# Queries and keys of three attention groups by seven products instead of eight

## The chip, the cores and the metric

One core of one Trainium2 chip. The metric is the device time of one execution in microseconds. TensorE (PE in the profile, its weight loads PEld), VectorE (DVE), ScalarE (ACT), GpSimd (POOL) and SyncE (SP) run side by side, each through its own queue in order, and wait for each other by semaphores.

## The reference

Two decoder layers over 256 tokens of width 2048. The change concerns the first one's differential attention:

```
q, k, v = split(h @ wqkv, 3)          # h: rms-normed x, wqkv: 2048 x 6144
q, k    = partial_rope(heads of 128)  # 16 heads, in 8 pairs
a       = softmax(q0 k0') - lam * softmax(q1 k1')   # per pair, causal
x       = x + rms_norm(a @ v, subln) * 0.2 @ wo
```

The second layer has multi-head latent attention. After each attention come a cross-attention into 256 memory tokens and a squared-ReLU feed-forward block of width 8192, and at the end a norm. All in float32.

## The kernel before, in words

**Precision.** Each float32 operand is split into two fp32r halves, and a product takes three matmuls: high x high, high x low, low x high. Weights come in tiles of 128x2048 floats (1 MB, pool `wraw`, tiles named `raw`, 6 buffers): 512 rows of the contraction by 512 columns. `split_pieces.next` makes of half such a tile `whi` (a cast on ScalarE, L193) and `wlo` (a subtraction on VectorE, L194). `whi` and `wlo` have 4 buffers each, so two weight tiles' worth of halves exist at a time.

**Activations** lie transposed in `unit` tiles (four 128-row pieces, both halves; 13 buffers). With 256 tokens there are two token blocks t = 0, 1. `matmul_chunk` computes 512 output columns for both blocks: 16 row pieces x 2 blocks x 3 = 96 matmuls, named `mm`.

**Attention in groups.** Differential attention runs in 4 groups of 512 columns (2 pairs of heads). `project_diff` takes the chunks for queries, keys and values; `heads_T` scales and rotates queries and keys (rotation on GpSimd, L454 to L459), transposes them on TensorE (L159) and splits them into `unit` tiles. `attend_diff` is a side task: for three blocks of scores it does softmax (L492) and weights (`a`, L631, L632), transposes these, multiplies by values, and then norms and transposes. While a group's side task runs, the main line does the output projection of the group before (`da_wo`, 4 tiles) and the projections of the group after (12 tiles).

**Order.** TensorE's order is as the program emits it. A model clock (`mmul` adds to it) decides between main-line matmuls which step of a side task is emitted: a task yields how long to wait (`T_SM` 6.5 us and so on), and `pump` emits steps that are due. A list `plan` sets the order of weight tiles, at most 4 ahead. The other engines' orders are set by a scheduler when the program is built. Weight loads go on SP's queue in the program's order.

**Seven products.** The feed-forward block's up projection already uses a Strassen-Winograd scheme (`Seven`): token blocks times halves of the contraction on one side, halves of the contraction times two chunks on the other, seven products p1 to p7 in place of eight, each of 8 row pieces x 3 = 24 matmuls (named `pr`) in two items x = 0, 1 of one weight tile. Sums of weights are made on VectorE (p5, p7; L758, 128x2048) or by a load that adds onto a tile, on GpSimd's queue (p6, p4; L764). Sums of activations s1 to s4 come from `Forms` (L412 sums, L384 and L385 halves). Outputs are put together on VectorE (L793). A product's item takes 12 matmuls, a plain one 24.

## Time and profile before

| | |
|---|---|
| median of 3 runs | 2247.61 us (2247.14 to 2247.9) |
| profiled execution | 2249.26 us, span 2247.5 us, granted clock 0.998 |
| PE busy | 2228.2 us, 99% |
| DVE busy | 1675.6 us, 75% |
| ACT busy | 1354.6 us, 60% |
| group 1, 62 to 153.5 us | PE 91.50, DVE 52.62, ACT 47.87 us busy |
| one feed-forward period, 620 to 704.4 us | PE 84.21, DVE 69.29, ACT 53.40 us busy |

The stretch from 62 us has the values of the first group, its attention and the projections of the second; those from 153.5 and 248 us the two groups after. In a row of a stretch stand its bounds and length, then busy time and number of instructions of PE, PEld, DVE, ACT and POOL, the granted clock, the share of the DMA engines and GB/s. A row of the timeline has start, duration, engine, line, operation, output and inputs, count, and in brackets the idle time before it and what ended it. A group row has count, busy time and mean duration in ns, then the idle time before.

### The profile page before, as it was taken

The page shows a single profiled execution, that of the slowest core. Times are in us where ns is not written, and L with a number is a line of the kernel's source. Part 1 is how long each engine was busy: PE and PEld are TensorE (multiplying, and loading weights), DVE is VectorE, ACT ScalarE, POOL GpSimd, SP SyncE. Part 2 cuts the span into 40 slices and gives each one's busy share as a digit, 9 for nine tenths or more (in the row PEclk, how much of TensorE's full clock was granted, in tenths as well). Part 3 has the DMA queues.
Part 4 walks back from the last instruction along what each step waited for, and adds up shares of the span by engine and source line. Part 5 has one row for each costly group of instructions (what it writes and reads, how often), then busy time and mean ns, then how long its engine had stood idle before and what let it go on. Part 6 is the DMA issues. An engine that isn't in the chain of part 4 may idle for free.

```text
span 2247.5 us, 27444 instructions
## 1 busy us (share of the span) xinstructions
PE 2228.2 (99%) x10521; PEld 1853.7 (82%) x10521; DVE 1675.6 (75%) x1836; ACT 1354.6 (60%) x1815; POOL 153.9 (7%) x250
## 2 busy tenths in 40 slices
PE   9999999999999999999999999999999999999998
PEld 7888888888888888888889888888888888888786
DVE  6665647678888788788765766778887887887864
ACT  6544645666666666656655755566666666666664
POOL 0210110000000000000000311000000000000001
PEclk9999999999999999999999999999999999999999
DMA  9446555435877877876955334643688678678692
GB/s 364 157 143 210 193 197 206 152 129 206 262 250 254 244 249 255 244 249 219 297 176 180 116 141 150 243 150 132 216 255 277 222 250 275 223 250 276 221 306 75
DMA packets 73716, 484.09 MB, mean 215 GB/s; under 512 B 8432, under 2 KB 8816, under 8 KB 18032
## 3 DMA queue, kind: packets, MB, share of 16 engines
q1 hardware_dynamic: 64944, 422.56, 50.9%
q0 software_dynamic: 8064, 58.72, 13.1%
q8 instruction: 82, 1.34, 0.2%
q10 hardware_dynamic: 576, 1.05, 0.2%
q14 instruction: 50, 0.41, 0.1%
HBM read 480.20 MB, written 2.10 MB: 215 GB/s over the span
## 4 chain that ended last, share of the span: by engine, by line
PE 92%; DVE 5%; ACT 2%; issue 1%; DMA 0%; ACTq 0%; POOLq 0%
PE mm L155 66%; PE pr L155 20%; PE ax L155 3%; PE ax L159 2%; DVE wlo L194 2%; DVE raw L758 2%; ACT whi L193 1%; PE mm L159 1%; DVE unit L289 0%; DMA raw<-in_da_wqkv_dram 0%; DVE x L438 0%; DVE unit L316 0%; ACT ev L1078 0%; DVE unit L487 0%; DVE os L658 0%
## 5 line engine op out<-in xcount | busy, mean ns | idle before, releaser
L194 DVE TENSOR_TENSOR wlo<-raw,whi 128x1024 fp32r<-128x1024 f32 (+2 forms) x962 | 1154.6, 1213 | 483.6 <-ACT whi L193 455.2
L193 ACT CAST whi<-raw 128x1024 fp32r<-128x1024 f32 (+2 forms) x962 | 993.6, 1041 | 754.5 <-PE mm L155 530.9
L155 PE MATMUL mm<-whi,unit 128*128 128x512 f32 (+3 forms) x4544 | 1444.0, 389 | 2.6 <-ACT unit L315 1.7
L155 PEld LDWEIGHTS mm<-whi,unit 128*128 128x128 f32 x4544 | 850.1, 188 | 169.2 <-ACT unit L315 2.7
L155 PE MATMUL mm<-wlo,unit 128*128 128x512 f32 (+3 forms) x2272 | 878.3, 387 | 2.2 <-DVE wlo L194 2.2
L155 PE MATMUL pr<-whi,unit 128*128 128x512 f32 x1568 | 502.9, 391 | 0.0
L155 PEld LDWEIGHTS mm<-wlo,unit 128*128 128x128 f32 x2272 | 428.0, 188 | 85.6 <-DVE wlo L194 7.2
L155 PEld LDWEIGHTS pr<-whi,unit 128*128 128x128 f32 x1568 | 294.4, 188 | 61.3 <-ACT whi L193 0.5
L155 PE MATMUL pr<-wlo,unit 128*128 128x512 f32 x784 | 307.3, 392 | 3.0 <-DVE wlo L194 2.7
L155 PEld LDWEIGHTS pr<-wlo,unit 128*128 128x128 f32 x784 | 147.2, 188 | 39.5 <-DVE wlo L194 9.5
L758 DVE TENSOR_TENSOR raw<-raw,raw 128x2048 f32<-128x2048 f32 x56 | 127.9, 2284 | 0.0
L764 POOL DMA_DIRECT2D raw<-in_mlp_wup_dram x56 | 49.4, 882 | 1125.6 <-DVE wlo L194 990.3
L438 DVE TENSOR_TENSOR x<-x,mm 128x512 f32<-128x512 f32 x152 | 100.0, 682 | 9.4 <-PE mm L155 8.7
L328 POOL TENSOR_TENSOR rs<-rs,mhalf 128x1 f32<-128x1 f32 (+1 forms) x28 | 23.5, 844 | 681.5 <-DVE rs L327 681.5
L288 ACT CAST unit<-ax 128x512 fp32r<-128x512 f32 (+1 forms) x88 | 48.9, 567 | 30.1 <-PE ax L159 27.7
L289 DVE TENSOR_TENSOR unit<-ax,unit 128x512 fp32r<-128x512 f32 (+1 forms) x88 | 57.4, 661 | 3.0 <-ACT unit L288 1.3
L500 ACT ACTIVATE p<-ax,nmax 128x256 f32<-128x256 f32 (+1 forms) x80 | 33.6, 428 | 30.0 <-DVE nmax L498 29.5
L322 ACT ACTIVATE junk<-x 128x512 bf16<-128x512 f32 x56 | 35.2, 628 | 9.4 <-DVE x L438 8.4
L155 PE MATMUL ax<-unit,unit 128*128 128x256 f32 (+1 forms) x240 | 37.2, 281 | 0.0
L155 PEld LDWEIGHTS ax<-unit,unit 128*128 128x128 f32 x240 | 34.3, 190 | 2.5
L155 PE MATMUL ax<-raw,unit 128*128 128x256 f32 (+1 forms) x240 | 35.3, 279 | 0.8 <-ACT unit L486 0.6
L155 PEld LDWEIGHTS ax<-raw,unit 128*128 128x128 f32 x240 | 32.0, 190 | 2.4 <-ACT unit L486 1.0
(150 smaller groups left out, 925.8 us busy)
## 6 DMA issues: line engine op xcount, KB each, us to landing
raw<-in_mlp_wup_dram SPq DMA_DIRECT2D x128, 1024.0 KB, 5.0
raw<-in_mlp_wdown_dram SPq DMA_DIRECT2D x128, 1024.0 KB, 7.0
raw<-in_mlp_wup_dram POOLq DMA_DIRECT2D x56, 1024.0 KB, 11.0
raw<-in_da_wqkv_dram SPq DMA_DIRECT2D x45, 1024.0 KB, 5.0
raw<-in_da_wo_dram SPq DMA_DIRECT2D x16, 1024.0 KB, 4.9
raw<-in_ca_wkv_dram SPq DMA_DIRECT2D x16, 1024.0 KB, 4.9
raw<-in_mla_wo_dram SPq DMA_DIRECT2D x16, 1024.0 KB, 5.0
raw<-in_ca_wq_dram SPq DMA_DIRECT2D x8, 1024.0 KB, 5.1
```

Source lines behind the costliest of these rows:

```text
L155: return nc.tensor.matmul(o, stationary, moving, start=start, stop=stop, skip_group_check=not alone)
L159: nc.tensor.transpose(o, src, ident)
L193: nc.scalar.copy(hi, r)
L194: nc.vector.tensor_tensor(lo, r, f32(hi), ALU.subtract)
L288: nc.scalar.copy(hi, src)
L289: nc.vector.tensor_tensor(dst[:, 1, :n, t * P : (t + 1) * P], src, f32(hi), ALU.subtract)
L322: nc.scalar.activation(junk[:, : src.shape[1]], src, AF.Square, accum_out=acc)
L328: nc.gpsimd.tensor_tensor(r[:, :n], r[:, :n], mhalf.broadcast_to([P, n]), ALU.pow)
L438: nc.vector.tensor_tensor(xc, xc, ps, ALU.add)
L500: nc.scalar.activation(pr[:, i * w : (i + 1) * w], sb[:, i * w : (i + 1) * w], AF.Exp, bias=nmax[:, i : i + 1], accum_out=ssum[:, i : i + 1],)
L758: tc.keep_in_program_order(nc.vector.tensor_tensor(o, o, other, ALU.add))
L764: add = nc.gpsimd.dma_start(o, self.source(*block, x), accum_op=ALU.add)
```

## The change

Queries and keys of groups 2 to 4 come from `Seven`: the two chunks (queries, keys) are its two output chunks. The first group stays as it was. `diff_line` interleaves the 14 items of the products with 8 plain items: in the first line the values of groups 1 and 2, later the output projection of the group before and the values of the next. `GivenForms` loads the given transposed x once more in four pieces, scales it by the gains on ScalarE, and forms s1 to s4 as a side task, begun behind the first group's keys; the forms that are no sums are read from the `unit` tiles that exist. They take four `unit` tiles and two `raw` tiles at times. `rotated_T` scales, rotates and transposes each product's output, and holds the transposes back until the running group's attention has been emitted. The steps of `attend_diff` after a softmax, after a transpose and after a norm become 3 us longer in groups 1 to 3 (`slack`), and one side bank of PSUM is withheld. The rest of the program is as before.

```diff
+    class GivenForms(Forms):
...
+        def sums(self):
+            for x in range(2):
+                rows = raw_tile().rearrange("p (k t) -> p k t", t=S)
+                for h in range(2):
+                    u = 2 * h + x
+                    load(rows[:, 4 * h : 4 * h + 4], self.src[:, 4 * u : 4 * u + 4, :])
+                    for i in range(4):
+                        row = rows[:, 4 * h + i]
+                        nc.scalar.activation(row, row, AF.Copy, scale=g[:, ...])
+                    yield T_TURN
+                self.sums_of(x, ...)       # 4 sums, 4 x (cast, subtraction)
+                yield T_SM
...
-            yield T_SM + 3.5
+            yield T_SM + 3.5 + slack
             pT = prob_T(a, 2, sb)
             give_back()
-            yield T_TURN
+            yield T_TURN + slack
+            while not v():
+                yield 0.5
...
+    def diff_line(gi):
+        values_of = lambda g: [("da_wqkv", 12 * g + 8 + u, CH) for u in range(4)]
+        others = values_of(0) if gi == 0 else [("da_wo", 4 * c + gi - 1, CH) for c in range(4)]
+        others = [Item(None, None, [job]) for job in others + values_of(gi + 1)]
+        seven = Seven("da_wqkv", 3 * (gi + 1)).items()
+        lead = 0 if gi else 2
+        line = others[:lead]
+        del others[:lead]
+        for n in (1, 1, 1, 1, 1, 2, 1) if gi else (1, 1, 0, 1, 1, 2, 0):
+            line += seven[:2] + others[:n]
+            del seven[:2], others[:n]
+        return line
...
+    def rotated_T(src, r, t, i, dst, free):
+        nc.scalar.activation(r, src, AF.Copy, scale=da_scales[i][t])
+        rope(r.rearrange("p (h d) -> p h d", h=4), *rotation(t))
+        def task():
+            yield T_ROT
+            while not free():
+                yield 0.5
+            b = yield from side_bank()
+            split(dst, t, transpose4(r, b))
...
-    norm, m, mk = attention(project_diff, ...)
+    forms = GivenForms(xT, acts, G_ATTN)
+    v, before, copied = [], None, {}
+    free_banks[0] -= 1
+    for gi, line in enumerate(diff_lines):
+        o = attend_group(q, k, v, 3.0)
+        nq, nk, nv = Held(unit()), Held(unit()), []
+        other = value_steps(v) if gi == 0 else output_steps(before)
+        other_then = value_steps(nv)
...
+        for item in line:
+            if item.of is not None:
+                item.of.products(forms, item.u, copied, produced)
+            elif next(other, 0) == 0:
+                next(other_then)
...
+    free_banks[0] += 1
+    o = attend_group(q, k, v, 0.0)
```

Three places show how instructions moved. In the changed kernel lines are shifted: L419 are the sums of activations, L389 their low halves, L787 the sums of weights, L473 the residual add, L533 the maximum, L540 and L660 the reciprocal and its factor, L666 and L667 the weights `a`.

VectorE in the first group, before: splits of value weights (`raw_615`, `raw_649`) and of the output weights, with the keys' transposes and the first softmax between them.

```order
L194 TENSOR_TENSOR wlo_622<-raw_615,whi_621 128x1024
L194 TENSOR_TENSOR wlo_652<-raw_649,whi_651 128x1024
L194 TENSOR_TENSOR wlo_656<-raw_649,whi_655 128x1024
L289 TENSOR_TENSOR unit_207<-mm_370,unit_207 128x4x128
L487 SCALAR_TENSOR_TENSOR unit_208<-mm_613,r_83_444,unit_208 128x512
L487 SCALAR_TENSOR_TENSOR unit_208<-mm_614,r_84_446,unit_208 128x512
L289 TENSOR_TENSOR unit_207<-mm_371,unit_207 128x4x128
L194 TENSOR_TENSOR wlo_698<-raw_695,whi_697 128x1024
L498 TENSOR_REDUCE nmax_821<-ax_807 128x4
```

The same place now: `unit_618` is s1, the form that p5 takes; `raw_743` are the second half's activations, `raw_755` is a value tile.

```order
L533 TENSOR_REDUCE nmax_873<-ax_859 128x4
L419 TENSOR_TENSOR raw_743<-raw_743 128x4x128
L194 TENSOR_TENSOR wlo_758<-raw_755,whi_757 128x1024
L194 TENSOR_TENSOR wlo_762<-raw_755,whi_761 128x1024
L419 TENSOR_TENSOR raw_743<-raw_743 128x4x128
L540 RECIPROCAL rsum_881<-ssum_874 128x4
L389 TENSOR_TENSOR unit_618<-raw_743,unit_618 128x512
L660 TENSOR_TENSOR rsum_881<-rsum_881,coef 128x4
L389 TENSOR_TENSOR unit_620<-raw_743,unit_620 128x512
```

The low half of s1 for x = 1 stands behind both splits of a value tile whose matmuls TensorE takes only after p5.

VectorE in the second group, before: the weights `a_1527` of the second softmax block, two splits behind the first block's.

```order
L194 TENSOR_TENSOR wlo_1369<-raw_1366,whi_1368 128x1024
L438 TENSOR_TENSOR x_82<-x_82,mm_1485 128x512
L505 RECIPROCAL rsum_1524<-ssum_1519 128x2
L438 TENSOR_TENSOR x_83<-x_83,mm_1486 128x512
L625 TENSOR_TENSOR rsum_1524<-rsum_1524,coef 128x2
L631 TENSOR_SCALAR a_1527<-p_1520,rsum_1524 128x256
L194 TENSOR_TENSOR wlo_1373<-raw_1366,whi_1372 128x1024
L632 SCALAR_TENSOR_TENSOR a_1527<-p_1520,rsum_1524,a_1527 128x256
```

Now: `raw_1595` and `raw_1558` are p3's tiles, which p7 makes its sums in; `raw_1624` is an output tile; `a_1720` are the second block's weights.

```order
L787 TENSOR_TENSOR raw_1595<-raw_1595,raw_1509 128x2048
L194 TENSOR_TENSOR wlo_1631<-raw_1624,whi_1630 128x1024
L194 TENSOR_TENSOR wlo_1682<-raw_1558,whi_1681 128x1024
L666 TENSOR_SCALAR a_1720<-p_1713,rsum_1717 128x256
L540 RECIPROCAL rsum_1768<-ssum_1763 128x2
L194 TENSOR_TENSOR wlo_1686<-raw_1558,whi_1685 128x1024
L549 TENSOR_TENSOR raw_1804<-ax_1640,raw_1804 128x256
L194 TENSOR_TENSOR wlo_1739<-raw_1595,whi_1738 128x1024
L473 TENSOR_TENSOR x_82<-x_82,mm_1807 128x512
L667 SCALAR_TENSOR_TENSOR a_1720<-p_1713,rsum_1717,a_1720 128x256
```

The weights are finished behind three splits of p7 and a residual add. On TensorE their transposes now stand inside the output item that is split as `wlo_1631`:

```order
L155 MATMUL mm_1807<-whi_1630,unit_622 128x512
L155 MATMUL mm_1807<-wlo_1631,unit_622 128x512
L155 MATMUL mm_1807<-whi_1630,unit_622 128x512 x2
L155 MATMUL mm_1807<-wlo_1631,unit_622 128x512
L155 MATMUL mm_1807<-whi_1630,unit_622 128x512
L159 MATMUL ax_1702<-identr,a_1720 128x128 x2
L155 MATMUL mm_1808<-whi_1630,unit_622 128x512
```

They come ahead of all of p7's matmuls, whose splits VectorE does first.

More of the change, by code (lines that the diff above doesn't have):

```diff
@@ L379, in form, with pieces @@
             return self.forms[key]
+        def pieces(self, key):
+            f = self.form(key)
+            return f.tasks, lambda half, kk: f[:, half, kk]
         def halves(self, key, x, src):
@@ L774, in products @@
             p, x = u
-            form = a.form(self.A[p])
-            need(form.tasks)
+            tasks, form = a.pieces(self.A[p])
+            need(tasks)
             onto = {"p2": "p1", "p3": "p5"}.get(p)
@@ L851, in mlp_line @@
             by = {p: [] for p in Seven.ORDER}
-            for item in Seven(l, b).items():
+            for item in Seven(f"mlp_wup{l}", 2 * b, b).items():
                 by[item.u[0]].append(item)
@@ L869, in trunk @@
     mlp_lines = {l: mlp_line(l) for l in range(2)}
+    def diff_line(gi):
[10 more added lines that the diff above has]
+        return line
+    diff_lines = [diff_line(gi) for gi in range(3)]
+    plan_k("da_wqkv", 8)
+    for line in diff_lines:
+        plan.extend(j for item in line for j in item.jobs)
+    plan_rows("da_wo", 2)
+    plan_k("ca_wkv0", 4)
+    plan_rows("da_wo", 3)
     plan_cross(0)
@@ new lines, in value_steps, with finish, output_steps @@
+    def value_steps(dst):
+        def finish(ps):
+            v = unit()
+            for t in range(NT):
+                values(ps[t], t, da_scales[1][t], v)
+            dst.append(v)
+        yield from chunk_steps(acts, finish)
+    def output_steps(o):
+        for c in range(4):
+            def finish(ps):
+                for t in range(NT):
+                    add_residual(t, c, ps[t])
+            yield from chunk_steps([o], finish)
+    def rotated_T(src, r, t, i, dst, free):
[7 more added lines that the diff above has]
+            split(dst, t, transpose4(r, b))
+            give_back()
+            yield T_TURN
+        dst.run(task())
@@ new lines, in trunk, with produced @@
+    forms = GivenForms(xT, acts, G_ATTN)
[6 more added lines that the diff above has]
+        other_then = value_steps(nv)
+        def produced(t, c, src, r, o=o, pair=(nq, nk)):
+            rotated_T(src, r, t, c, pair[c], lambda: all(task.done for task in o.tasks))
+        for item in line:
[3 more added lines that the diff above has]
+                next(other_then)
+        next(other_then, 0)
+        if gi == 1:
+            mem_norm()
+        q, k, v, before = nq, nk, nv, o
@@ L1176, in trunk @@
+    free_banks[0] += 1
+    o = attend_group(q, k, v, 0.0)
+    m = []
+    project_group(before, each=lambda c: m.append(given_unit(memT, c, G_MEM)))
+    mk = mem_keys(m)
+    norm = Stream(G_CROSS)
+    project_group(o, norm)
     norm = cross(0, norm, m, mk)
```

89 lines of the change are left out of this document (50 added, 39 removed).

## The prediction

> **What bounds the kernel now.** I read the page's engine and chain lines first, then the stretches of the three groups that change beside one period of the feed-forward block, which already runs seven products, then who TensorE waits for.
>
> ```profile
> PE 2228.2 (99%) x10521; PEld 1853.7 (82%) x10521; DVE 1675.6 (75%) x1836; ACT 1354.6 (60%) x1815; POOL 153.9 (7%) x250
> PE mm L155 66%; PE pr L155 20%; PE ax L155 3%; PE ax L159 2%; DVE wlo L194 2%; DVE raw L758 2%; ACT whi L193 1%; PE mm L159 1%; DVE unit L289 0%; DMA raw<-in_da_wqkv_dram 0%; DVE x L438 0%; DVE unit L316 0%; ACT ev L1078 0%; DVE unit L487 0%; DVE os L658 0%
> 62.00:153.50 91.50, 91.50 (x448) 76.81 (x447) 52.62 (x68) 47.87 (x74) 15.93 (x39) 1.00 0.49 173
> 153.50:248.00 94.50, 94.39 (x451) 78.89 (x450) 57.79 (x79) 49.98 (x84) 10.58 (x28) 1.00 0.55 190
> 248.00:344.50 96.50, 96.50 (x463) 80.79 (x462) 57.69 (x74) 46.62 (x71) 9.46 (x26) 1.00 0.50 175
> 620.00:704.40 84.40, 84.21 (x378) 69.05 (x377) 69.29 (x62) 53.40 (x59) 3.49 (x4) 1.00 0.78 250
> PE mm L155 <- DVE wlo L194: 0.2, 1, 0.2
> ```
>
> TensorE carries the time: 99% busy, 92% of the chain. In the first three stretches (one group of attention each; columns: us, then PE, PEld, DVE, ACT, POOL, clock, DMA) it never rests while VectorE is busy 58 to 61%. In the feed-forward period (fourth stretch) VectorE is at 82%, and TensorE's only wait there (last row) is 0.2 us. So a matmul taken away is time gained as long as VectorE keeps ahead; whether it does in these groups is the whole question.
>
> **What is taken away.** Two chunks, queries and keys, cost 2 x 96 matmuls of 512 columns a group; seven products cost 14 x 12 = 168. Three groups lose 72. The steady pitch:
>
> ```profile
> 547.65 5.44 PE pr L155 x24
> 80.73 1.51 PE ax L155 x13
> 86.44 0.88 PE ax L155 x8
> 113.57 0.44 PE ax L159 x4
> ```
>
> 24 in 5.44 us is 0.227 each: 72 x 0.227 = **16.3 us** off TensorE. Transposes and scores stay as many, about 0.11 us each.
>
> **What is added on VectorE.** An item of the seven products feeds 12 matmuls (2.72 us) where one item fed 24 (5.44 us), but is split into halves like any other. A group has 14 + 8 items in place of 16: 44 splits for 32. Added further: four sums of 128x2048, five of 128x512 to form the outputs, and in the first group 16 instructions of 128x512 for the sums of activations. Prices, from one dense run and from rows of like shape:
>
> ```profile
> 503.83 1.22 DVE L194 TENSOR_TENSOR wlo<-raw,whi 128x1024 fp32r<-128x1024 f32 x1
> 504.97 0.69 DVE L412 TENSOR_TENSOR raw<-raw 128x512 f32<-128x512 f32 x1
> 505.57 0.22 DVE L334 TENSOR_REDUCE tot<-ss 128x1 f32<-128x4 f32 x2
> 618.93 2.28 DVE L758 TENSOR_TENSOR raw<-raw,raw 128x2048 f32<-128x2048 f32 x1
> 621.13 2.35 DVE L194 TENSOR_TENSOR wlo<-raw,whi 128x1024 fp32r<-128x1024 f32 x2
> L498 DVE TENSOR_REDUCE nmax<-ax 128x2 f32<-128x512 f32 x6 | 4.1, 690 | 0.4 <-PE ax L155 0.3
> L487 DVE SCALAR_TENSOR_TENSOR unit<-mm,r,unit 128x512 fp32r<-128x512 f32 x6 | 4.3, 744 | 0.0
> L514 DVE TENSOR_TENSOR raw<-ax,raw 128x256 fp32r<-128x256 f32 x9 | 3.8, 419 | 0.3 <-ACT raw L513 0.3
> L632 DVE SCALAR_TENSOR_TENSOR a<-p,rsum,a 128x256 f32<-128x256 f32 x6 | 2.9, 480 | 0.1
> L505 DVE RECIPROCAL rsum<-ssum 128x2 f32<-128x2 f32 x6 | 1.0, 159 | 0.8 <-ACT p L500 0.8
> ```
>
> Back to back, start to start is about 0.08 us under the duration: 1.14 for a split, 2.20 for a long sum, 0.60 for 512 columns, and by the same rebate 0.61, 0.66, 0.34, 0.40 and 0.07 for the last five rows. The second group then holds 44 x 1.14 + 4 x 2.20 + 5 x 0.60, eight residual adds and four key and query halves at 0.60, two value halves at 0.66, and some 10 us of softmax and norm: 80.5 us, against 94.5 - 5.4 = 89 of TensorE. That is 90%, where the feed-forward period has 82%.
>
> On average it fits. It does not everywhere, since the halves have four buffers (half an item each): VectorE may write a half only after TensorE's last matmul on the half four before, and then through ScalarE:
>
> ```profile
> 62.20 0.39 PE L155 MATMUL mm<-whi,unit 128*128 128x512 f32 x1
> 62.68 1.05 ACT L193 CAST whi<-raw 128x1024 fp32r<-128x1024 f32 x1 [1.66 <-PE mm L155]
> 63.76 1.23 DVE L194 TENSOR_TENSOR wlo<-raw,whi 128x1024 fp32r<-128x1024 f32 x1 [1.39 <-ACT whi L193]
> ```
>
> From the matmul's slot end (62.20 + 0.23) to the low half written (64.99) are 2.55 us. Four halves of seven products are only 5.4 us of TensorE. So I take stretches: from TensorE's last use of a buffer, 2.55 us plus all VectorE work in its order up to what TensorE needs next, against the matmuls between.
>
> *First group:* from the last matmul on the second value item to the transposes of the third softmax block. VectorE's order there has 18 splits (20.5), 4 long sums (8.8), 15 of 128x512 (9.0), 3 maxima (1.8), 2 value halves (1.3) and the small rows of three softmax blocks (3.1): 44.5, with the handover 47.1. TensorE has 145 x 0.227 + 18 x 0.118 + 28 x 0.109 = 38.0. **Wait 9.0 us.** About half of it falls at the second half of p5, whose sum of activations stands in VectorE's order behind a value split two items on (the order shown above).
>
> *Second group:* from the last matmul before the first line's p4 to the transposes of the second softmax block, which stand behind a split of p7 and a residual add. VectorE: 21 splits (23.9), 4 long sums (8.8), 13 short (7.9), the rest 2.4: 42.9, with the handover 45.5. TensorE: 163 x 0.227 + 12 x 0.118 + 30 x 0.109 = 41.6. **Wait 3.9.**
>
> *Third group:* the same reckoning on its tightest piece, around p3, up to the third block's transposed weights, gives 16.5 + 2.55 against 18.4: **0.7**. Elsewhere I find VectorE ahead.
>
> How unsure is it? A free run (no waits) costs 0. If every one of the 105 VectorE instructions of the two stretches pays its whole row instead of the rebate, 105 x 0.08 = 8.5 us come on top. I take the dense pitch, since a run such as that from 503.83 holds it across many kinds of rows.
>
> **What I cost at nothing.** ScalarE:
>
> ```profile
> L193 ACT CAST whi<-raw 128x1024 fp32r<-128x1024 f32 (+2 forms) x962 | 993.6, 1041 | 754.5 <-PE mm L155 530.9
> L315 ACT ACTIVATE unit<-raw,g 128x256 fp32r<-128x256 f32 x32 | 13.9, 499 | 0.0
> L384 ACT CAST unit<-raw 128x512 fp32r<-128x512 f32 x14 | 8.3, 620 | 1.1 <-DVE raw L412 0.7
> raw<-in_da_wqkv_dram SPq DMA_DIRECT2D x45, 1024.0 KB, 5.0
> raw<-in_mlp_wup_dram POOLq DMA_DIRECT2D x56, 1024.0 KB, 11.0
> DMA to landing us min/median/max: 8.8/11.0/15.0
> ```
>
> It gains 12 casts (12.5 us) and two copies a group, and 16 x 0.50 + 8 x 0.62 = 13 us in the first: at most 48 + 27 = 75 of 89 us. Its in-order links with VectorE can still cost tenths. Loads on SP: eight a group as before, plus four halves of the activations in the first; a 1 MB load lands in 5.0 us, and each freed buffer is refilled at least 10 us of work ahead. Four adding loads a group come on POOL's queue, issued behind VectorE's splits and between the rotations. The tight one is from p6 to p4: 15 us of TensorE between their first uses, less 2.5 of handover and about 1.5 of POOL rows ahead, leaves 11: 11.0 is just hidden; at 15.0 it costs 4 in a group. What waits behind it on POOL are rotations, needed 10 us later. I take 0 and keep 4 x 3 for the upper end. The longer steps put three attention blocks 3 us further down TensorE's line; the tail of each group has the next group over it, and the last keeps its old steps and its cover of 43 us of projections.
>
> **Sum.** The profiled execution took 2249.26 us (span 2247.5), 1.65 over the median of 2247.61. 2249.26 - 16.3 + 9.0 + 3.9 + 0.7 = 2246.6; against the median 2244.9, taken as **2245.0**. Nearly all of the gain turns into waits for VectorE. What this kernel's runs can tell from no change is about 0.2%, 4.5 us.
>
> **Rivals.**
> *No waits*, as in the feed-forward block: 2247.6 - 16.3 = 2231.3. For it speaks the 0.2 us row; against it the 44.5 us in a place of 38.
> *Waits in part:* the second and third groups hide theirs and the first pays 6 to 9: 2237 to 2241. For it: the second group's excess is only 3.9 of 45, and an order that lets VectorE start one item earlier removes it.
> *Slower:* VectorE's stretches do not run dense, because splits, sums and casts of ScalarE take turns: 8.5 us more, 2253.4. It decides once each of the 105 instructions loses over 0.07 us (7.2 us, 2252.1). For it: single splits behind a cast pay 1.23 (63.76). Against: the run from 503.83.
> *The clock falls in the waits.* After TensorE's first start the pitch was half as fast:
>
> ```profile
> 0.00:40.00 40.00, 37.05 (x143) 27.13 (x144) 23.47 (x37) 25.10 (x43) 0.20 (x4) 0.96 0.96 367
> 9.67 0.71 PE L155 MATMUL mm<-whi,unit 128*128 128x512 f32 x1 [1.38 <-ACT unit L315]
> 10.17 0.63 PE L155 MATMUL mm<-wlo,unit 128*128 128x512 f32 x1
> 13.16 0.66 PE L155 MATMUL mm<-whi,unit 128*128 128x512 f32 x2
> 13.66 0.39 PE L155 MATMUL mm<-wlo,unit 128*128 128x512 f32 x1
> ```
>
> Steps of about 0.43 us (10.17 follows 9.67 by 0.50; by 13.16 two take 0.50) last 3.5 us, which costs 1.7. If a wait of 4 us brings that on, the first group absorbs it (VectorE catches up meanwhile) and the second pays 1.7: 2246.7. The Trainium skill, "TensorE: Matmul & The Clock Gate", section "HAM oscillation — how this bites in real kernels", warns of gaps over about 3.4 us between bursts, after which TensorE runs at half rate; by that rule the sum would be this one. No wait in this trace is long enough to show it.
>
> **Numbers.** Forecast (waits of 11.8 to 20.8 us, clock case included): 0.45, the likeliest, 2243 to 2252, within 0.2%. Waits in part 0.26 and none 0.10: faster, 0.36. Slower 0.19. The range leaves out the case of no waits and the far half of the slow one: 2236 to 2255.
>
> **What would show it.** Right: 10449 matmuls; TensorE's waits named as VectorE (sums, splits) of 8 to 10 us in the first group and 3 to 5 in the second, next to none in the third; VectorE near 10 tenths just there; the feed-forward stretches unchanged. Wrong: no wait at p5, or waits on ScalarE, loads, or adding loads before p4; a granted clock under 1.00 in groups one and two would speak for the clock case.

## Result, and the profile after

The changed kernel takes 2259.61 us (median of 6 runs, 2255.81 to 2261.64) against 2247.44 before (6 runs): ratio 1.0052, 95% interval 1.0039 to 1.0065. It is slower by 12 us, where 2245 was forecast and 2255 was the upper end. The profiled execution took 2261.25 us, span 2259.1.

From the page of the kernel after, the engines' busy time and the chain by engine (TensorE had 92% of the chain before):

```profile
PE 2221.2 (98%) x10449; PEld 1843.3 (82%) x10449; DVE 1758.1 (78%) x1915; ACT 1401.6 (62%) x1881; POOL 198.9 (9%) x262
PE 87%; DVE 7%; ACT 2%; DMA 2%; issue 1%; POOL 1%; ACTq 0%; POOLq 0%; DVEq 0%
```

The 72 matmuls are gone. Where the time went is read from two stretches: up to the first adding load of the feed-forward block (the same point of both programs, 570.2 us before and 581.8 after), and 60 to 440 us. Before:

```profile
0.00:570.20 570.20, 565.93 (x2689) 469.04 (x2690) 382.18 (x531) 326.82 (x525) 49.34 (x117) 1.00 0.55 196
60.00:440.00 380.00, 379.55 (x1837) 317.77 (x1836) 244.33 (x340) 204.87 (x337) 41.41 (x102) 1.00 0.53 184
```

After:

```profile
0.00:581.80 581.80, 559.28 (x2617) 458.83 (x2618) 465.15 (x610) 373.54 (x591) 94.94 (x129) 0.99 0.65 218
60.00:440.00 380.00, 361.21 (x1711) 297.57 (x1711) 320.90 (x411) 245.36 (x395) 85.94 (x112) 0.98 0.67 216
```

The point comes 11.6 us later, which is the whole loss: the rest of the program takes as long as before. TensorE rests 570.20 - 565.93 = 4.3 us before and 22.5 after, 18.3 more. And its busy time falls by 6.6 us only (565.93 to 559.28), not by the 16.3 of 72 matmuls: it runs slower for a while. GpSimd's busy time doubles in 60 to 440 us, though its rotations are about as many; only 12 issues of adding loads (10.8 us) are new.

TensorE's longest waits there, from the timeline in order of time (in brackets the rest and what ended it). The first line is the list of items that runs over group 1's attention:

```profile
79.02 0.50 PE L155 MATMUL pr<-whi,unit 128*128 128x512 f32 x1 [1.61 <-ACT whi L193]
80.28 0.50 PE L155 MATMUL pr<-wlo,unit 128*128 128x512 f32 x1 [0.76 <-DVE wlo L194]
90.73 0.59 PE L155 MATMUL pr<-whi,unit 128*128 128x512 f32 x1 [4.46 <-ACT unit L388]
161.84 0.50 PE L155 MATMUL pr<-wlo,unit 128*128 128x512 f32 x1 [0.68 <-DVE wlo L194]
166.91 0.50 PE L155 MATMUL pr<-wlo,unit 128*128 128x512 f32 x1 [2.02 <-DVE wlo L194]
178.71 0.66 PE L159 MATMUL ax<-identr,u 128*128 128x128 f32 x4 [3.56 <-POOL u L494]
207.52 0.69 PE L159 MATMUL ax<-identr,a 128*128 128x128 f32 x2 [3.57 <-DVE a L667]
```

The first two are p5's first half, the third its second half (s1 is late), the next two p4's halves, the transposes of the query rotated last, and the transposes of the second softmax block in the second line. VectorE was full ahead of p5: between 62 and 110 us its waits come to 2.0 us in 48, and this is the longest:

```profile
DVE rsum L540 <- ACT p L535: 1.0, 1, 1.0
```

What ended the wait of 4.46 us was ScalarE, though (a sum on VectorE first, then ScalarE's rows):

```profile
85.47 0.68 DVE L419 TENSOR_TENSOR raw<-raw 128x512 f32<-128x512 f32 x1
86.31 1.04 ACT L193 CAST whi<-raw 128x1024 fp32r<-128x1024 f32 x1 [1.00 <-PE pr L155]
87.37 1.28 ACT L535 ACT_TABLE_LOAD   x1
90.06 1.15 ACT L388 CAST unit<-raw 128x512 fp32r<-128x512 f32 x2
```

The sum for s1 was ready at 86.15 us, before TensorE's rest began at 86.27. The cast that makes its high half (L388) began only at 90.06, because in ScalarE's order it stands behind a cast of weights, a table load of 1.28 us and the first softmax block.

Ahead of p4, VectorE had a wait of its own, for an adding load that was issued at 139.38 us and took 14.1 us to land:

```profile
153.56 1.05 ACT L193 CAST whi<-raw 128x1024 fp32r<-128x1024 f32 x1 [4.90 <-DMA raw<-in_da_wqkv_dram]
154.64 1.23 DVE L194 TENSOR_TENSOR wlo<-raw,whi 128x1024 fp32r<-128x1024 f32 x1 [4.62 <-ACT whi L193]
```

**The clock.** Four stretches, one behind each of the rests at 79 to 80, 91, 179 and 207 us (the seventh column after the bounds, 0.50, is the granted clock):

```profile
80.80:84.20 3.40, 3.40 (x13) 2.92 (x13) 3.40 (x5) 3.40 (x7) 0.00 (x0) 0.50 0.56 149
91.00:94.40 3.40, 3.40 (x9) 2.42 (x9) 3.40 (x10) 1.65 (x3) 0.00 (x0) 0.50 0.52 217
179.70:183.10 3.40, 3.40 (x10) 2.63 (x9) 1.19 (x2) 1.33 (x2) 0.00 (x0) 0.51 0.45 186
207.10:210.50 3.40, 2.98 (x8) 2.48 (x9) 1.70 (x5) 0.37 (x1) 0.00 (x0) 0.51 1.00 178
```

Each lasts 3.4 us. In the first three TensorE is busy throughout and loses half of it, 1.7 us; in the last it still rests for 0.4 us and loses 1.5: 6.6 us in all. So 16.3 are gained, 18.3 rested off and 6.6 lost to the clock; 3.0 of the 11.6 remain. An estimated 1.8 of these come from how a rest is counted: from the end of a matmul's row, 0.39 us behind its start, where the next matmul could have started after 0.23. That is 0.16 us for each of the eleven rests between 79 and 308 us. No row accounts for the other 1.2.

The four stretches start at 80.76, 91.00, 179.74 and 207.05 us, which are 3, 26 and 8 times 3.413 us apart. Here are four windows of that grid; the first number behind the length is TensorE's busy time:

```profile
77.34:80.76 3.42, 1.05 (x4) 0.62 (x4) 3.02 (x3) 3.42 (x6) 0.00 (x0) 1.00 0.49 201
162.68:166.09 3.41, 2.22 (x10) 1.48 (x8) 3.41 (x4) 1.92 (x3) 1.60 (x1) 1.00 0.00 0
166.09:169.51 3.42, 2.60 (x11) 2.17 (x12) 3.42 (x4) 1.92 (x3) 3.42 (x1) 1.00 0.00 0
176.33:179.74 3.41, 1.03 (x7) 0.95 (x8) 1.87 (x2) 0.34 (x1) 2.33 (x2) 1.00 0.89 312
```

TensorE rested for 2.4 us of the first and of the last, and the half clock followed. The rest of 2.02 us that ended at 166.91 lies across two windows, with 1.2 us of rest in one and 0.8 in the other, and nothing followed. Counted in this way in the traces of all 17 runs, half clock followed each of the 22 full-clock windows with 2.0 us of rest or more, 7 of the 22 with 1.4 to 1.9 us, and none with less.

**The rotation.** GpSimd and VectorE before the transposes at 178.71:

```profile
163.44 2.28 DVE L787 TENSOR_TENSOR raw<-raw,raw 128x2048 f32<-128x2048 f32 x1
164.49 9.30 POOL L489 TENSOR_TENSOR rope<-u,cos 128x64 f32<-128x64 f32 x1 [12.20 <-ACT u L1241]
165.64 4.62 DVE L194 TENSOR_TENSOR wlo<-raw,whi 128x1024 fp32r<-128x1024 f32 x4
170.18 2.29 DVE L787 TENSOR_TENSOR raw<-raw,raw 128x2048 f32<-128x2048 f32 x1
172.38 1.22 DVE L194 TENSOR_TENSOR wlo<-raw,whi 128x1024 fp32r<-128x1024 f32 x1
173.52 1.28 DVE L473 TENSOR_TENSOR x<-x,mm 128x512 f32<-128x512 f32 x2
174.70 3.68 POOL L493 TENSOR_TENSOR u<-rope,rope 128x64 f32<-128x64 f32 x1
174.71 3.49 DVE L194 TENSOR_TENSOR wlo<-raw,whi 128x1024 fp32r<-128x1024 f32 x3
178.34 0.31 POOL L494 TENSOR_TENSOR u<-rope,rope 128x64 f32<-128x64 f32 x1
```

A GpSimd instruction that takes 0.32 us elsewhere took 9.30. It began within a run of VectorE instructions that each read two operands from SBUF, and ended 0.27 us into the first one that reads only one there (L473; its other operand is in PSUM). The next such run held L493 for 3.68.

### The profile page after: what moved, and what is told of

Read it like the earlier page. It is cut to its first block, busy times and chain, and to the rows that moved or that the text cites. A ratio compares the mean times of both kernels' runs of the same rounds, so it can differ in the third digit from the quotient of the medians.

```text
span 2259.1 us, 27535 instructions
## 1 busy us (share of the span) xinstructions
PE 2221.2 (98%) x10449; PEld 1843.3 (82%) x10449; DVE 1758.1 (78%) x1915; ACT 1401.6 (62%) x1881; POOL 198.9 (9%) x262
## 4 chain that ended last, share of the span: by engine, by line
PE 87%; DVE 7%; ACT 2%; DMA 2%; issue 1%; POOL 1%; ACTq 0%; POOLq 0%; DVEq 0%
PE mm L155 59%; PE pr L155 23%; DVE wlo L194 3%; PE ax L155 3%; PE ax L159 2%; DVE raw L787 2%; ACT whi L193 2%; DMA raw<-in_da_wqkv_dram 1%; PE mm L159 1%; DVE unit L289 0%; POOL rope L489 0%; DVE unit L522 0%; DMA raw<-in_xT_dram 0%; DVE x L473 0%; ACT raw L451 0%
## 5 line engine op out<-in xcount | busy, mean ns | idle before, releaser
L194 DVE TENSOR_TENSOR wlo<-raw,whi 128x1024 fp32r<-128x1024 f32 (+3 forms) x998 | 1195.5, 1212 | 412.3 <-ACT whi L193 382.5
L193 ACT CAST whi<-raw 128x1024 fp32r<-128x1024 f32 (+3 forms) x998 | 1029.4, 1041 | 705.3 <-PE mm L155 439.8
L155 PE MATMUL mm<-whi,unit 128*128 128x512 f32 (+3 forms) x4160 | 1325.0, 389 | 2.5 <-ACT unit L315 1.6
L155 PEld LDWEIGHTS mm<-whi,unit 128*128 128x128 f32 x4160 | 778.3, 188 | 154.1 <-ACT unit L315 2.4
L155 PE MATMUL mm<-wlo,unit 128*128 128x512 f32 (+3 forms) x2080 | 803.5, 386 | 3.0 <-DVE wlo L194 2.9
L155 PE MATMUL pr<-whi,unit 128*128 128x512 f32 x1904 | 616.7, 393 | 6.1 <-ACT unit L388 4.5
L155 PEld LDWEIGHTS mm<-wlo,unit 128*128 128x128 f32 x2080 | 391.9, 188 | 80.4 <-DVE wlo L194 8.9
L155 PEld LDWEIGHTS pr<-whi,unit 128*128 128x128 f32 x1904 | 359.1, 189 | 81.4 <-ACT unit L388 4.9
L155 PE MATMUL pr<-wlo,unit 128*128 128x512 f32 x952 | 374.8, 394 | 7.1 <-DVE wlo L194 6.8
L155 PEld LDWEIGHTS pr<-wlo,unit 128*128 128x128 f32 x952 | 179.7, 189 | 52.4 <-DVE wlo L194 16.4
L787 DVE TENSOR_TENSOR raw<-raw,raw 128x2048 f32<-128x2048 f32 x68 | 155.2, 2283 | 0.0
L473 DVE TENSOR_TENSOR x<-x,mm 128x512 f32<-128x512 f32 x152 | 99.7, 680 | 9.1 <-PE mm L155 8.5
```

Of the source, the lines that this page charges most:

```text
L155: return nc.tensor.matmul(o, stationary, moving, start=start, stop=stop, skip_group_check=not alone)
L193: nc.scalar.copy(hi, r)
L194: nc.vector.tensor_tensor(lo, r, f32(hi), ALU.subtract)
L473: nc.vector.tensor_tensor(xc, xc, ps, ALU.add)
L787: tc.keep_in_program_order(nc.vector.tensor_tensor(o, o, other, ALU.add))
```

## Experiments

The theory at the outset, A: four separate waits and the clock's fall behind each. Its main rival is B: VectorE's work over the whole line is too much, and a wait removed comes back elsewhere. C, D, L and V are other rivals; each expectation says what its letters stand for. All ratios are to the kernel before, which was run again beside every experiment (medians 2247.33 to 2247.82 us). In the edits `...` marks code left out, and words behind `#` are remarks.

### Without seven products in the first line

```diff
+        plain = [("da_wqkv", 12 + u, CH) for u in range(8)] if gi == 0 else []
+        others = [Item(None, None, [job]) for job in others + plain + values_of(gi + 1)]
+        if gi == 0:
+            return others                  # sixteen plain items
         seven = Seven("da_wqkv", 3 * (gi + 1)).items()
...
```

> Queries and keys of the second group are made as before (two chunks of 96 matmuls, 24 more than with seven products), in a first line of sixteen plain items; the sums of activations are still made behind the first keys, and groups three and four keep their seven products. Theory A (four separate waits of 2.4 to 4.5 us, three of them in the first line, each followed by 3.4 us at half clock): the three waits of the first line and their three clock falls go, the wait of 3.6 us and its clock fall in the second line stay. 2247.4 - 2 x 5.44 + 3.6 + 1.7 = 2242, within 2. Theory B (VectorE and ScalarE cannot carry the sums and seven products, and the delay only moves): the second line inherits a delay and 2248 or more comes out.

Measured 2242.89 us, ratio 0.998 (0.9971 to 0.9989): within A's range, and faster than before. TensorE's waits from 55 to 440 us come to 4.6 us; the longest kinds are:

```profile
PE pr L155 <- DVE wlo L194: 2.3, 2, 1.3
PE ax L155 <- DVE raw L549: 1.6, 2, 1.2
```

Nothing is over 1.3 us, and there is no half clock in these groups. So A met the time by luck: it had left the wait of 3.6 us in the second line and its clock fall standing, 5.3 us, and both went. That VectorE enters this line less late without the products in the first is a guess.

### The rotation: on VectorE, or given more time

```diff
-        rope(r.rearrange("p (h d) -> p h d", h=4), *rotation(t))            # GpSimd
+        rope(r.rearrange("p (h d) -> p h d", h=4), *rotation(t), nc.vector)
```

> The rotations of the queries and keys made by seven products run on VectorE instead of GpSimd (24 instructions of 128x64 a group, some 0.13 us each, 3 us of VectorE a group); all else as in the changed kernel. Theory A (a GpSimd instruction with two operands in SBUF is held as long as VectorE runs such instructions back to back, 9.3 us for one of 0.32): TensorE's wait of 3.6 us for the rotation in the first line and its clock fall go, 2259.6 - 5.3 = 2254, at most 3 us given back by the fuller VectorE: 2254 to 2257. Theory B (VectorE's total work is what TensorE waits for): 3 us more of it in each line make the waits longer, 2262 or more.

```diff
-            yield T_ROT
+            yield T_ROT + 8.0
             while not free():
```

> The transposes of the rotated queries and keys stand 8 us later in TensorE's order (20 us behind the product in place of 12); nothing else. Theory A: the rotation is late by 3.6 us at one place, so the later place hides it and the clock does not fall there: 2259.6 - 3.6 - 1.7 = 2254. Theory B: TensorE meets the same late VectorE at the next split, and the time stays 2259.

2254.30 us, ratio 1.0032 (1.0020 to 1.0045), and 2253.94, ratio 1.0029 (1.0018 to 1.0040): both as A has it, 5.3 and 5.7 us under the changed kernel. B's figure for the first (2262 or more) failed: VectorE took on 72 instructions, and the time fell. On VectorE such an instruction takes 0.22 us:

```profile
L490 DVE TENSOR_TENSOR rope<-u,cos x3: 217/218/219, 165.0 to 349.2; 128x64 f32<-128x64 f32 x3
```

In the second of the two, the waits that are left from 160 to 215 us are VectorE's alone:

```profile
PE ax L159 <- DVE a L667: 2.6, 1, 2.6
PE pr L155 <- DVE wlo L194: 1.3, 1, 1.3
```

2.6 + 1.3 = 3.9. So the rotation's wait was a cost of its own. Whether it also made VectorE later is not shown: the wait of the second softmax block fell from 3.57 us to 2.64 here, but grew to 4.01 in the first of the two.

### The clock: rests filled with idle matmuls

```diff
+    def fill_in(o, n):
+        for _ in range(n):                 # n matmuls of 512 columns, result unused
+            nc.tensor.matmul(o.rearrange("p (a b) -> p a b", a=2), identr, acts[0].tile[:, 0, 0:2], start=True, stop=True)
...
+            if line_at[0] == 0 and p == "p5":
+                fill_in(bank(), (8, 12)[x])          # first try; (8, 20)[x] in the second
...
```

> Matmuls without use (512 columns, 0.227 us each) are put into TensorE's order just ahead of the four places where it waited: 8 and 12 ahead of the first and second half of p5 in the first line, 10 ahead of the late rotated query, 10 ahead of the second softmax block's transposes in the second line (9.1 us in all). They shorten the rests to under 2.5 us and change no other engine's work. Theory A (each rest of over about 2.4 us costs 3.4 us at half clock behind it, a loss of 1.7): no half clock in groups one and two, 2259.6 - 4 x 1.7 = 2252.8. Theory C (the time regained is only waited off again, as VectorE is the bound): clock 0.998 but 2259 again. If the fillers come on top of the waits: up to 2268.

> As the filled kernel before, with more matmuls without use: 8 and 20 ahead of the halves of p5, 10 ahead of the second half of p4, 12 ahead of the rotated query, 14 ahead of the second softmax block in the second line (14.5 us in all), so that hardly a rest over 1 us is left in these places. No other engine's work changes. Theory A (the clock falls because TensorE rests, at 2.0 us already in some cases): clock as in the kernel before (0.998), and the four losses of 1.7 us gone: 2253. Theory C (TensorE is held by VectorE whatever its clock): 2258 or more with the same clock.

The first: 2257.39 us, ratio 1.0043 (1.0031 to 1.0056), 2.2 us gained where 6.8 were expected. Its profiled execution, the slowest of the five (2253.85 to 2259.87), shows a part of why: rests of 2.01 us at 87.4 and 2.03 at 164.7 were left, and behind each the clock was at half for 3.4 us. Besides, its 40 fillers (9.1 us) and the 15.0 us of rests left up to the first adding load of the feed-forward block make 24.1 us, against 22.5 in the changed kernel.

The second: 2256.10, ratio 1.0033 (1.0021 to 1.0046), between A's figure and C's. In its profiled execution, the fastest of the five (2253.08 to 2256.39), no half clock is left but in the last microseconds of the program, and at the common point of the programs (573.9 us):

```profile
0.00:573.90 573.90, 565.26 (x2681) 465.24 (x2682) 465.43 (x610) 373.96 (x591) 88.62 (x129) 1.00 0.65 221
```

That is 7.9 us before the changed kernel, with the same work on VectorE. 1.3 us of it were gained at the start, where the clock fell in the changed kernel (9.1 to 12.5 us) and not here: a split that begins at 30.52 us there begins at 29.25 here, ahead of any filler. The 64 fillers are 14.5 us; with the 8.6 us of rests left this makes 23.1, against 22.5 of rests in the changed kernel. So in this execution filling made no wait shorter, and the other 6.6 us are the clock's, as many as were reckoned above.

The median gained only 3.5 us, and not because the clock fell again in the slower executions: all five have a granted clock of 0.998 or 0.999, the changed kernel's six 0.995 or 0.996. In those, part of what the clock gave must have been lost elsewhere, in waits or in fillers; only one execution was profiled, so where stays open.

### Where the wait ahead of p5 comes from

Three kernels. The first moves the plain items, the second leaves out the sums of activations, the third only their second load:

```diff
-        lead = 0 if gi else 2                                 # e5
+        lead = 0 if gi else 4
-        for n in (1, 1, 1, 1, 1, 2, 1) if gi else (1, 1, 0, 1, 1, 2, 0):
+        for n in (1, 1, 1, 1, 1, 2, 1) if gi else (1, 1, 0, 1, 0, 1, 0):
-                self.sums_of(x, ...)                          # e9
-                for h in range(2):                            # e13
+                for h in range(0 if x else 2):
```

> In the first line all four value items stand ahead of p1 (two in the changed kernel), and the plain items behind it are spread one for every one or two products; nothing else. Theory A: the sums of activations have 10.9 us more of matmuls ahead of p5, so the waits at its two halves (2.4 and 4.5 us) and the two clock falls behind them (1.7 each) go: 2259.6 - 10.3 = 2249, and up to 3 more for a fuller stretch behind: 2249 to 2252. Theory B (the work of VectorE over the whole line is too much): the waits move to p3 to p4 and the time stays within 2 of 2259.6.

> The eight sums of activations and their high and low halves (in the first line 16 instructions of 128x512 on VectorE and 8 casts on ScalarE) are left out, p3, p5, p6 and p7 take plain halves of the activations; the loads of the activations for them and their scaling on ScalarE stay. Theory A (the second half of p5 waits for those sums; the rest of the first line waits for VectorE): the wait of 4.5 us and its clock fall go (6.2), and with 9 us less on VectorE some of the other waits of the first line: 2253 if none of them, 2246 if all but the one behind the late load. Theory C (sums and casts do not matter, the late load of activations does): 2256 or more.

> The second load of activations for the sums and its scaling on ScalarE are left out (two loads of 512 KB, eight activations of 128x256); the second half of the sums is made from the rows of the first, so VectorE's 16 instructions and ScalarE's 8 casts stay. Theory L (p5 waits because that load is late and what ScalarE casts stands behind it): both waits at p5 and their clock falls go, 6.9 + 3.4 us: 2249, 2247 to 2252. Theory V (VectorE's order of splits and sums makes p5's second half late in any case): only the first wait goes, the second keeps 3 us or more: 2254 to 2258.

**Four values first:** 2261.27 us, ratio 1.0060 (1.0048 to 1.0073). A is wrong here and B right. There is no wait at p5, but one of 3.45 us at 101.1 us for the softmax weights behind VectorE, and others follow up to 158 us:

```profile
PE ax L159 <- DVE a L667: 7.5, 2, 4.0
PE pr L155 <- ACT whi L193: 4.9, 3, 2.6
```

The second row is a cost that the forecast had at nothing: with fewer plain items between the products, ScalarE's casts wait for the adding loads of p6 and p4: 15.0 us for three of them, which took 11.6 to 16.7 us to land. Up to the same 180 us it is 7.5 us for two in the changed kernel.

```profile
ACT whi L193 <- DMA raw<-in_da_wqkv_dram: 15.0, 3, 6.6
```

**No sums of activations:** 2252.27 us, ratio 1.0021 (1.0013 to 1.0030), within A's bounds: 7 us less for 9 us of VectorE's work, with two half-clock stretches in these groups in place of four.

**Second half unloaded:** 2259.44 us, ratio 1.0048 (1.0034 to 1.0062). In the changed kernel ScalarE's order held 4.6 us for that load just ahead of p5's casts, which looked like a cause:

```profile
76.32 1.71 ACT L451 ACTIVATE raw<-raw,g 128x256 f32<-128x256 f32 x4 [4.61 <-DMA raw<-in_xT_dram]
```

It isn't what the time hangs on: without the load it is the same. The rest of 4.46 us at p5 is gone, and 2.75 us at 79.5 and 1.63 + 1.06 + 0.76 at 103 to 110 us came in its place, all for the halves of weights. VectorE has a single wait from 62 to 110 us there, of 0.8 us.

L fell, and V's figure did too: the waits stand at other places, but their sum is nearly the same (6.2 us, 7.4 in the changed kernel). With VectorE full in that stretch, this fits that its work there sets the sum, whichever engine ends a single wait.

### VectorE's sums of weights

```diff
-                if other is not None:
+                if other is not None and self.b is not None:   # feed-forward block only
                     tc.keep_in_program_order(nc.vector.tensor_tensor(o, o, other, ALU.add))
```

> The four sums of weights of a group (128x2048 on VectorE, 2.2 us each) are left out in groups two to four: their splits take the raw weights, the adding loads stay. Theory A: VectorE's dense runs at p4 of the first line and before the second softmax block of the second line end, so the wait for p4 (2.7), for the rotation (3.6), for the weights of the softmax (3.6) and two clock falls (3.4) go; the wait at p5's first half, behind a late load of activations on ScalarE, and that at its second half stay at least in part: 2259.6 - 13.3 = 2246, 2240 to 2249. Theory C (the added loads, banks or ScalarE carry the waits): 2255 or more.

2237.79 us, ratio 0.9956 (0.9944 to 0.9968): 21.8 us under the changed kernel, and below A's range (2240 to 2249). All that is left of TensorE's waits from 55 to 440 us:

```profile
PE ax L155 <- DVE unit L289: 1.6, 1, 1.6
PE mm L155 <- DVE wlo L194: 1.4, 2, 0.8
PE pr L155 <- DVE wlo L194: 0.7, 1, 0.7
```

Even the waits at p5 and for the rotation are gone, and no half clock is left in these groups. So with 12 sums (26 us of VectorE) less, 18.5 us of waits become 3.7. This does not tell VectorE's time from the order of steps: without a sum, ScalarE's cast of the same tile need not wait for it either (9.8 us of such waits in the changed kernel). No run separates the two.

### The sums by adding loads

```diff
+                added = self.ADDED if self.b is not None else {**self.ADDED, "p1": ("p1", (0, 1)), "p3": ("p3", (0, 1))}
...
-        for n in (1, 1, 1, 1, 1, 2, 1) if gi else (1, 1, 0, 1, 1, 2, 0):
+        for n in (2, 0, 2, 1, 0, 2, 1) if gi else (2, 0, 2, 0, 0, 2, 0):     # e10, e11
+        for n in (2, 1, 2, 0, 1, 2, 0) if gi else (1, 1, 0, 1, 1, 2, 0):     # e15
```

> The weight sums of p5 and p7 are made by adding loads (as those of p6 and p4 already are) and not on VectorE: eight adding loads a group for four, two plain loads and four sums of 128x2048 fewer. Two plain items stand behind p1, p3 and p6, so that an adding load has at least 10.9 us of matmuls to land. Theory A (VectorE's work in dense places decides): nearly the time without those sums, 2238, and up to 8 more where adding loads, which need 8 to 17 us to land, are late for p5, p7 or p6: 2238 to 2246. Theory C (adding loads wait on one queue and take the place of the sums as the wait): 2255 or more.

> The same adding loads with a plain first line: seven products only for groups three and four. Theory A: 2247.6 - 2 x 5.44 = 2236.7 if nothing waits; 2242.9 was measured with the sums on VectorE, where TensorE's waits in the lines of seven products came to about 4 us. 2237 to 2241. Theory C (late adding loads): 2244 or more.

> Seven products for groups three and four, weight sums of p5 and p7 by adding loads, with plain items also between p5 and p3 (whose bank must be copied first, the 1.7 us waits of the first try) and two behind p1, p3 and p6; the memory's norm at the end of the first line. Theory A: the two waits of 1.7 us for the copies and the split behind the memory's squares go: 2246.8 - 4.4 = 2242 or less, down to 2237. Theory C (late adding loads for p7 to p4 limit it): 2244 or more.

2265.88 us, ratio 1.0079 (1.0065 to 1.0093); 2246.78, ratio 0.9998 (0.9990 to 1.0007); 2245.48, ratio 0.9991 (0.9983 to 1.0000). The second and the third have the plain first line as well, the third also the memory's norm a line earlier. All miss A's range, in the sense of C. In the first of them:

```profile
PE pr L155 <- ACT p L832: 9.2, 3, 5.6
PE pr L155 <- DVE wlo L194: 4.6, 8, 1.0
```

p3 adds onto p5's bank, which ScalarE must first copy (L832); with nothing between p5 and p3 that copy is waited for. The third, which has a plain item there, lost those waits and got others of 1.67 and 1.17 us for casts at 266 to 271 us, and from 266.7 us on the clock was at half for 10.2 us. Taking the sums off VectorE helps only if nothing slower takes their place.

### The attention steps, and three edits at once

```diff
-        o = attend_group(q, k, v, 3.0)
+        o = attend_group(q, k, v, 0.0)                          # e7
+        o = attend_group(q, k, v, 7.0 if gi == 1 else 3.0)      # e8, with lead 4 and T_ROT + 8
```

> The attention steps of groups one to three get back the distances of the kernel before (slack 0 in place of 3); nothing else. Theory A: the transposes of the softmax weights stand 3 us earlier in TensorE's order, while VectorE is as late as before: the wait of 3.6 us in the second line grows by up to 3, others of its kind appear: 2260 to 2266. Theory D (the longer steps push work into the dense places and cost time): 2256 or less.

> All three at once on the changed kernel: four value items ahead of p1, the rotated queries and keys transposed 8 us later, and the attention steps of the second line 4 us longer still (slack 7). Theory A, by the sum of the waits and clock falls that each removes: 2259.6 - 10.3 - 5.3 - 5.3 = 2238.7, 2236 to 2244, under the kernel before. Theory B (VectorE's total bounds these groups): no lower than 2250.

The steps as before: 2258.88 us, ratio 1.0053 (1.0041 to 1.0066), no difference from the changed kernel's 1.0052. Neither theory's figure came; the rotation's wait is not there, and others, 2.0 and 2.2 us among them, stand at the attention's places. The three edits: 2260.99, ratio 1.0060 (1.0046 to 1.0073), 22 us over A's sum. **Theory A fell here:** its waits don't add up. A shortage of VectorE that shows wherever TensorE next meets it, as B has it, fits this run and the one with four values first; the rotation's wait alone was a separate cost.

### The plain first line, tuned

On top of the plain first line:

```diff
-        if gi == 1:
+        if gi == 0:
             mem_norm()
...
-        o = attend_group(q, k, v, 3.0)
+        o = attend_group(q, k, v, 6.0)
```

> The plain first line (seven products for groups three and four only), the norm of the memory (eight squares of 128x512 on ScalarE and their small rows) moved from the end of the second line to the end of the first, and attention steps 3 us longer still (slack 6 for groups one to three). Theory A: of the 4.6 us of waits that the plain first line still had, the two of the second line's end (2.3, splits behind the memory's squares) and those of attention (1.6) go: 2242.9 - 3.9 = 2239, 2237 to 2241. If the memory's squares only move the wait into the first line, or slack does nothing: 2242 to 2244.

2240.97 us, ratio 0.9973 (0.9963 to 0.9984): faster than both kernels, by 6.4 us against the one before, of 10.9 that 48 matmuls are worth.

```profile
60.00:440.00 380.00, 377.29 (x1823) 313.79 (x1822) 304.93 (x401) 240.92 (x388) 65.32 (x105) 1.00 0.64 211
```

There are 2.7 us of rests in 380, and the clock is at 1.00. The step from the plain first line alone (2242.89) is 1.9 us, and the two intervals overlap; which of the two further edits did it is not separated.

## Why the prediction was wrong, step by step

**What is taken away, 16.3 us: right.** 10521 became 10449 matmuls. In the filled execution TensorE, without the fillers, is busy for 565.3 - 14.5 = 550.8 us, 15.2 less than before; a part of that is the start, where the clock fell in the kernel before and not there.

**VectorE in dense stretches: the sum nearly right, the way only in part.** For the first group 9.0 us were forecast; up to the transposes of the third softmax block 1.61 + 0.76 + 4.46 + 0.57 = 7.4 came. Half of it did fall at p5's second half, but not as told: the forecast had a half of s1 late in VectorE's order, and the trace has its cast late in ScalarE's, behind a table load and the softmax. ScalarE was put at nothing, and waits on it were named as a sign of being wrong. So the place and the size were met partly by luck. For the second group 3.9 were forecast; the changed kernel has 0.68 + 2.02 + 3.57 = 6.3, and 3.9 in one execution where the rotation is given time. For the third 0.7; 0.41 came. That VectorE's sums carry these waits is shown by the run without them. The forecast's objection to the slow rival, that VectorE runs dense, held as well (2.0 us of waits in 48).

**The clock, at nothing in the sum: failed.** The prediction has it in a rival, "if a wait of 4 us brings that on", at 1.7 us for one place. It fell at four places, 6.6 us. The trace of before had shown it already, at the place that the prediction took for TensorE's start:

```profile
6.37:9.78 3.41, 1.69 (x6) 0.60 (x5) 1.64 (x3) 1.68 (x4) 0.00 (x0) 1.00 0.96 320
9.78:13.20 3.42, 3.42 (x9) 2.57 (x10) 3.18 (x9) 3.29 (x8) 0.00 (x0) 0.50 1.02 407
```

The clock was full up to 9.78 us. TensorE was at rest for 1.7 us of the window ahead (its longest rest there is 1.38), and then the clock halved. So "No wait in this trace is long enough to show it" was wrong. The reason given for a small cost, that the first group absorbs its share because VectorE catches up meanwhile, fails in the profiled filled execution, which got the 6.6 us back; by the medians 3.5 came back, so a part may be absorbed. The rule of the Trainium skill, "TensorE: Matmul & The Clock Gate", section "HAM oscillation — how this bites in real kernels" (gaps over about 3.4 us), was on the right side, and the measurement is stricter: 4.46, 3.56 and 3.57 us brought the half clock, but so did 1.61 and 0.76 us together, and 2.01 and 2.03 in the filled kernel, while 2.02 at 166.9 did not.

**GpSimd's rotations, "needed 10 us later", at nothing: failed.** They cost 3.6 us of rest and one of the four clock falls, 5.3 us, and two experiments agree (5.3 and 5.7 measured). The 10 us of cover were counted right; what was missing is that the rotation itself needs 14 us when VectorE is dense. The trace of before hinted at it, next to a row that the prediction quotes (the split at 63.76, 1.23 us):

```profile
63.75 1.41 POOL L458 TENSOR_TENSOR ev<-rope,rope 128x64 f32<-128x64 f32 x1
132.83 0.33 POOL L459 TENSOR_TENSOR ev<-rope,rope 128x64 f32<-128x64 f32 x1
```

The same instruction's shape takes 0.33 alone and 1.41 beside one split. A table of durations by shape, as was made for VectorE, would have shown that it is held up, though not that it can take 9.30.

**Loads and longer steps at nothing: nearly right, but for one adding load.** Taking the late load of activations away changed nothing, and the steps' old distances neither. The prediction's "at 15.0 it costs 4 in a group" nearly came: one adding load took 14.1 us, and VectorE stood 4.62 us behind it, ahead of the dense run in which p4's splits came late. p4's waits are 2.7 us there, and 1.0 and 1.1 in the two runs in which VectorE stood under 2 us at a time at this place (rotations on VectorE; the steps as before). In the variants with more adding loads, or with less between them, such loads became the wait.

**The sum.** 13.6 us of waits were forecast and 18.3 came; of the 4.7 over, 3.6 are the rotation's. The clock adds 6.6, which the sum had at nothing. So the rotation and the clock are the terms that failed. Of the 3.0 us left, 1.8 are an estimate from how rests are counted, and 1.2 stay unexplained. The forecast case and the slow rival (2253.4) were both off, for reasons that neither had.

## What to carry to other kernels

Where matmuls are taken away by giving VectorE more work, find the stretch in which VectorE is full, and put the change only where a line has room: two of the three groups gain 6 us (with a norm moved and longer steps), all three lose 12. Price a rest of TensorE at its length and, where 2 us of rest fall into one 3.41 us window, at up to 1.7 us more for the clock behind it; with 1.4 to 1.9 us it may come, with less it never came here. A wait removed at one place of an over-full stretch can come back at the next, so test by taking work away before moving it. Read every engine's order at the place that matters: at p5 the last to be ready was not the fullest engine.

## What was not expected of the hardware

- An instruction of 0.32 us on GpSimd took 9.30 us beside seven VectorE instructions with two SBUF operands, back to back; it came through as soon as one with a PSUM operand ran. The Trainium skill, "SBUF — State Buffer", section "Who interferes with whom", says that a VectorE instruction with two SBUF inputs contends with a GpSimd instruction that reads SBUF; the trace agrees, and shows that one GpSimd instruction can be held across several of VectorE's in a row. At other places it came through between two splits: beside one run of four splits (130.6 to 135.5 us) two of its instructions got a turn one after the other:

```profile
130.63 4.88 DVE L194 TENSOR_TENSOR wlo<-raw,whi 128x1024 fp32r<-128x1024 f32 x4
132.42 0.74 POOL L489 TENSOR_TENSOR rope<-r,cos 128x64 f32<-128x64 f32 x1 [5.47 <-ACT r L1241]
133.13 1.30 POOL L490 TENSOR_TENSOR rope<-r,sin 128x64 f32<-128x64 f32 x1
```

What decides it is open.
- The half clock came in pieces of 3.41 us on one grid of such windows in each trace, and what counted was how much rest fell into one window: a rest of 2.02 us across two windows did not bring it, and 1.61 and 0.76 us in one did. Whether it comes at 1.4 to 1.9 us stays open (7 of 22).
